# Queueing each product by V one softmax step later in a two-mixer encoder layer

## The chip, the cores and the metric

The kernel runs on one core of a Trainium2 chip. The metric is the device time of one execution in microseconds (us); less is better. All times below are of that core.

## What is computed

One encoder layer over 1024 frames of width 1024, with two token mixers, each with 8 heads of width 64. Mixer A is banded: a block of 128 queries sees at most 640 keys, with a learned bias. Mixer B is chunk-causal with a rotary part: the block of queries number i sees (i + 1) x 128 keys. Cut to what matters:

```python
# mixer A, per head and chunk
s = q @ k.T * scale + bias;  p = softmax(s);  y = p @ v
# mixer B, per head and block of 128 queries
s = q_full @ k_full.T * scale;  s = where(mask, s, -1e30);  p = softmax(s);  y = p @ v
# around them: projections of the layer's input, gates, output
ya = (y_A * silu(z_A)) @ w_proj_a
yb = (y_B * silu(z_B)) @ w_proj_b
out = (sigmoid(g_A) * ya + sigmoid(g_B) * yb) @ w_out, then a residual and a layer norm
```

## The kernel before, in words

The attention of a mixer is cut into 64 steps: 8 heads by 8 blocks of 128 queries, heads two by two in four "pairs", mixer A first (steps with `m` = 0), then mixer B (`m` = 1). One step (`Steps.one`) has these parts:

- `scores`: TensorE multiplies queries by keys into a tile of PSUM (pool `ps_sc`, two buffers); lines L692 and L693 for A, L789 to L791 for B. For A a step has 2 matmuls when i is under 4 and 4 otherwise; for B 3 and 6. VectorE moves the tile to SBUF and finds the row's extreme (L697 for A, L796 for B).
- `softmax`: ScalarE takes the exponential (L808), VectorE the reciprocal of the sum (L810, L811), ScalarE writes the upper half of the weights as fp16 (L815), VectorE the rest as a second fp16 part (L816). A transposing DMA, issued from SyncE (SP), brings both parts into a tile `pT` (L818).
- `pv`: the product by V. TensorE multiplies `v16` by `pT` (L830), two matmuls for each 128 keys of the step: 2, 4, 6, 8 and then 10 for A, 2 to 16 for B. They gather in a tile `y`, which holds four steps; after the fourth, `finish_y` evacuates it (L721, L722, L728) and stores it (L730).

The product by V of a step is not made in that step. `Steps` keeps a queue `q`; `fin` takes the oldest entry. With a lag of 3 (`LAG_A`) in A and 2 (`LAG_B`) in B, step s ends with the product of step s - 3 or s - 2. The pool of `pT` has lag + 1 buffers, so four in A and three in B. Besides, A has three buffers each for the scores in SBUF and for the fp16 weights, B two.

The steps are mixed with "dense" work: `run` interleaves the stream of steps with the stream of the big projections (`Chunk.mm`, six matmuls of 512 columns a unit, names `dn<-hT`, helper lines L167 to L169), by the share of each stream's cost that is done; the steps lead by a factor of 1.25. The order in which the program is written is a priority and not the final order: a planner puts each engine's instructions into a queue at compile time, taking the first in program order among those which it reckons to be ready. On the chip each engine works its queue off in that order, and waits on semaphores.

Between heads, `next_head` (at i = 6) starts the loads of the next head: the swapped queries `sX`, for A the bias tile `tb`, for B the rotary queries `qr`, of which there is one buffer. After A, `drain` makes the products that are left; after B the list `fins` does, interleaved with the projection of A (`proj_a`, name `pj`).

Of the kernel before, what the change touches and what calls it, by code (L numbers as in the profile page):

```python
# [18 lines left out]
P = 128  # L19
# [14 lines left out]
LAG_B = 2  # L34
# [21 lines left out]
def tile_hybrid_layer(  # L56
# [27 lines left out]
    T = nc.tensor  # L84

    def f(ap):
        return ap.bitcast(F32)
# [116 lines left out]
    def start_ya():  # L204

        if not YA:
            tiles = {}

            def one(k, half):
                if (k // 2, 0) not in tiles:  # L210
                    for a in range(2):
                        tiles[k // 2, a] = m8.tile([P, 2, S], F32R, tag="m8", name=f"YA{k // 2}{a}")
                for a in range(2):
                    YT[0][a] = YT[0][a] or {}
                    YT[0][a][k] = tiles[k // 2, a][:, k % 2, :]
                y_part(0, k, half, YT[0][0][k], YT[0][1][k])

            YA.extend([(0, lambda k=k, half=half: one(k, half)) for k in range(4) for half in range(2)])
        return YA

    def start_yb():

        t = [big.tile([P, 4, S], F32R, tag="big", name=f"YB{a}") for a in range(2)]
        for a in range(2):
            YT[1][a] = {k: t[a][:, k, :] for k in range(4)}
        return [(0, lambda k=k, half=half: y_part(1, k, half, YT[1][0][k], YT[1][1][k])) for k in range(3) for half in range(2)]
# [400 lines left out]
    with ExitStack() as p1:  # L627
# [24 lines left out]
        class PairA:  # L652
# [31 lines left out]
            def scores(self, e, i):  # L684
                h = 2 * self.p + e
                k0 = max(0, i - 4)
                n = (i - k0 + 1) * P
                ps = ps_sc.tile([P, 2, 512], F32, tag="sc", name=f"sa{h}_{i}")
                nb, w = (1, max(n, 256)) if n <= 512 else (2, n // 2)
                for b in range(nb):  # L690
                    ks = slice(k0 * P + b * w, k0 * P + b * w + w)
                    T.matmul(ps[:, b, :w], self.sQ[e][:, i * P : (i + 1) * P], self.sK[e][:, ks], start=True, stop=False)  # L692
                    T.matmul(ps[:, b, :w], self.sX[e][:, i * P : (i + 1) * P], self.sK[e][:, ks], start=False, stop=True)  # L693
                w = min(w, n)
                s = pools["s"].tile([P, 640], F32, tag="s", name=f"ss{h}_{i}")
                nm = sm.tile([P, 1], F32, tag="nm", name=f"nm{h}_{i}")
                V.tensor_tensor_reduce(  # L697
                    s[:, :n].rearrange("p (b w) -> p b w", b=nb),
                    ps[:, :nb, :w],
                    self.tb[e][:, 640 - n : 640].rearrange("p (b w) -> p b w", b=nb),  # L700
                    -0.125, 3e38, ALU.add, ALU.min, nm,
                )
                return s, nm, n
# [30 lines left out]
        class PairB:  # L734
# [46 lines left out]
            def scores(self, e, i):  # L781
                h = 2 * self.p + e
                n = (i + 1) * P
                ps = ps_sc.tile([P, 2, 512], F32, tag="sc", name=f"sb{h}_{i}")
                nb, w = (1, max(n, 256)) if n <= 512 else (2, n // 2)
                qs = slice(i * P, (i + 1) * P)
                for b in range(nb):
                    ks = slice(b * w, b * w + w)
                    T.matmul(ps[:, b, :w], self.sQ[e][:, qs], self.sK[e][:, ks], start=True, stop=False)  # L789
                    T.matmul(ps[:, b, :w], self.sX[e][:, qs], self.sK[e][:, ks], start=False, stop=False)  # L790
                    T.matmul(ps[:, b, :w], self.qr[e][:, qs], krt[:, ks], start=False, stop=True)  # L791
                w = min(w, n)
                V.memset(ps[0:64, nb - 1, w - 64 : w], NEG)
                s = pools["s"].tile([P, S], F32, tag="s", name=f"sbs{h}_{i}")
                nm = sm.tile([P, 1], F32, tag="nm", name=f"nmb{h}_{i}")
                V.tensor_scalar(  # L796
                    s[:, :n].rearrange("p (b w) -> p b w", b=nb), ps[:, :nb, :w], -B_SCALE, None,
                    op0=ALU.mult, op1=ALU.min, accum_out=nm,
                )
                return s, nm, n  # L800
# [1 line left out]
            def tail(self, e, half, yt, r):  # L802
                finish_z(self, 1, e, half, yt, r)

        def softmax(pair, e, i, nm_):
            s, nm, n = pair.scores(e, i)
            su = sm.tile([P, 1], F32, tag="su", name=f"su{nm_}")
            A.activation(s[:, :n], s[:, :n], AF.Exp, scale=-1.0, bias=nm, accum_out=su)  # L808
            rc2 = sm.tile([P, 1], F32, tag="rc2", name=f"rcs{nm_}")
            V.tensor_scalar(rc2, su, 2.0 ** -14, None, op0=ALU.mult)  # L810
            V.reciprocal(rc2, rc2)  # L811
            W_ = pools["w"]
            p16 = pools["p"].tile([P, 2 * W_], F16, tag="p16", name=f"p16{nm_}")
            hi, lo = p16[:, :n], p16[:, n : 2 * n]
            A.activation(hi, s[:, :n], AF.Copy, scale=rc2)  # L815
            V.scalar_tensor_tensor(lo, s[:, :n], rc2, hi, op0=ALU.mult, op1=ALU.subtract)  # L816
            pT = pools["pt"].tile([P, 2 * W_ // P, P], F16, tag="pt", name=f"pT{nm_}")
            SY.dma_start(pT[:, : 2 * n // P, :], p16[:, : 2 * n], transpose=True)  # L818
            return pT
# [18 lines left out]
        class Steps:  # L838
# [7 lines left out]
            def one(self):  # L846
                pair, e, i = self.seq[self.at]
                self.at += 1
                nm = f"{self.m}_{2 * pair.p + e}_{i}"
                self.q.append((pair, e, i, softmax(pair, e, i, nm)))  # L850
                if i == 6:
                    self.next_head()
                if len(self.q) > self.lag:
                    self.fin()

            def next_head(self):
                n = self.at + 1
# [70 lines left out]
        def att_pools(es, w, lag):  # L928
            pools["w"] = w
            for nm, bufs in (("s", 3 if w == 640 else 2), ("p", 3 if w == 640 else 2), ("pt", lag + 1)):  # L930
                pools[nm] = es.enter_context(tc.tile_pool(name=f"at_{nm}{w}", bufs=bufs, **rt))

        def at(units, where):

            out_ = []
            for i, u in enumerate(units):
                for w, more in where:
                    if w == i:
                        out_ += more
                out_.append(u)  # L940
            for w, more in where:
                if w >= len(units):
                    out_ += more
            return out_
# [21 lines left out]
        with ExitStack() as pb:  # L966
            att_pools(pb, S, LAG_B)
            pools["qr"] = pb.enter_context(tc.tile_pool(name="at_qr", bufs=1, **rt))
            krt = pools["qr"].tile([96, S], F32R, tag="kr", name="krt", bufs=1)
            for b, part in enumerate((0, 1, 0)):  # L970
                SY.dma_start(f(krt[32 * b : 32 * b + 32, :]), kr_d[part])
            pairsB[0].load_qr(0)
            sb = Steps(1, pairsB, LAG_B)
            for p in range(4):
                u = sb.units(16)
                if p < 3:
                    n = pairsB[p + 1]
                    extra = [(1 + j, [x_]) for j, x_ in enumerate(vb1[1])] if p == 0 else []
                    if p == 1:
                        extra = [(j, [x_]) for j, x_ in enumerate(vb1[2]())]  # L980
                    if p == 2:
                        extra = [(12 + j, [x_]) for j, x_ in enumerate(start_ya()[:4])]
                    u = at(u, extra + [(6, [(0, n.prep_w)]),
                               (PL[0], [(1.3, lambda n=n: n.prep_k(0))]), (PL[1], [(1.3, lambda n=n: n.prep_k(1))]),
                               (PL[2], [(1.3, lambda n=n: n.prep_q(0))]), (PL[3], [(1.3, lambda n=n: n.prep_q(1))])])
                    run(u, dense((5, 6, 5)[p]))
                else:
                    run(at(u[:5], [(j, [x_]) for j, x_ in enumerate(start_ya()[4:])]), dense(1))
                    yb = start_yb()
                    fins = [(0.5, sb.fin)] * LAG_B  # L990
                    run(at(u[5:] + fins, [(3 + j, [x_]) for j, x_ in enumerate(yb)]), proj_a(range(0, 6)))
            for _, fn in proj_a(range(6, 8)):
                fn()
# [94 lines left out]
    for j in range(NT):  # L1088
        n = 4 if j == last else 2
# [68 lines left out]
```

## Time and profile before

| what | value |
|---|---|
| median of 3 runs | 881.63 us (877.91 to 886.0) |
| profiled execution | 881.12 us |
| its span, first to last instruction | 879.3 us |
| mean granted clock of TensorE, as a share of full | 0.984 |
| attention of A, first scores to last product by V | 165.7 to 390.7 us |
| attention of B, first scores to last product by V | 377.0 to 725.9 us |

The profile shows one execution. PE is TensorE's matmuls, PEld its weight loads, DVE VectorE, ACT ScalarE, POOL GpSimd, SP SyncE with the DMA queue. A matmul's record ends at a modelled time; the next one often starts before that. A bracket behind a row holds the engine's idle time just before it and what ended that. A clock of 1.00 is 2.4 GHz, 0.50 is 1.2 GHz.

### The profile page before, as it was taken

Reading aid. Unit: us, or ns where it says so; the run is one execution under the profiler, and the core shown is the slowest. Engines: PE = TensorE matmul, PEld = TensorE weight load, DVE = VectorE, ACT = ScalarE, POOL = GpSimd, SP = SyncE. Lnnn points to the kernel's source line nnn. Section 1 sums busy time; section 2 is a strip of 40 time slices with the busy share of each in tenths; the row PEclk is TensorE's granted clock in tenths of the full one; section 3 lists DMA queues with packets and bytes.
Section 4 is the critical chain, followed back from the end, with each engine's and each line's share of the span. In section 5 each row is a group of like instructions: output and inputs, shape, how many; then the busy total and the mean of one; then the engine's idle time right before and its main releaser. Section 6 shows DMA issues by size and latency. Waiting matters only on the chain. (4 is left out here: it accounts for less than half of the span.)

```text
span 879.3 us, 13755 instructions
## 1 busy us (share of the span) xinstructions
PE 827.7 (94%) x4760; PEld 693.2 (79%) x4760; DVE 554.0 (63%) x1267; ACT 441.9 (50%) x857; POOL 299.6 (34%) x285
## 2 busy tenths in 40 slices
PE   4899799999998997899999999999999899999996
PEld 4899798887777775787787877888888778778886
DVE  6899765577667678846555645166527563557754
ACT  4233465377576756847553755366647452322000
POOL 5646642222232222712122732122344334541100
PEclk9999999999999998999999999999999899999998
DMA  6632103467878774685676566546877797541421
GB/s 193 207 120 76 37 24 96 152 131 149 171 136 178 143 147 108 121 195 117 138 159 154 128 142 144 162 106 150 212 186 181 153 220 255 184 149 59 146 96 48
DMA packets 185365, 124.68 MB, mean 142 GB/s; under 512 B 146160, under 2 KB 149744, under 8 KB 185296
## 3 DMA queue, kind: packets, MB, share of 16 engines
q1 hardware_dynamic: 185296, 123.82, 57.7%
q8 instruction: 37, 0.61, 0.3%
q14 instruction: 32, 0.26, 0.1%
HBM read 57.98 MB, written 22.81 MB: 92 GB/s over the span
## 5 line engine op out<-in xcount | busy, mean ns | idle before, releaser
L167 PE MATMUL dn<-hT,wh_c 128*128 128x512 f32 x512 | 204.7, 400 | 2.1 <-DVE bQ L640 1.0
L169 PE MATMUL dn<-hT,wl_c 128*128 128x512 f32 x512 | 201.3, 393 | 0.0
L168 PE MATMUL dn<-hT,wh_c 128*128 128x512 f32 x512 | 200.8, 392 | 0.0
L132 POOL TENSOR_TENSOR wl_c<-wr_c,wh_c 128x512 fp32r<-128x512 f32 x64 | 83.9, 1310 | 226.8 <-ACT wh_c L131 214.5
L167 PEld LDWEIGHTS dn<-hT,wh_c 128*128 128x128 f32 x512 | 96.7, 189 | 20.2 <-DVE bQ L640 1.4
L169 PEld LDWEIGHTS dn<-hT,wl_c 128*128 128x128 f32 x512 | 96.4, 188 | 19.7
L168 PEld LDWEIGHTS dn<-hT,wh_c 128*128 128x128 f32 x512 | 96.7, 189 | 17.5
L816 DVE SCALAR_TENSOR_TENSOR p<-sbs,rcs,p 128x128 f16<-128x128 f32 (+3 forms) x64 | 57.1, 898 | 28.3 <-ACT p L815 27.8
L728 POOL TENSOR_TENSOR yt<-yt,sz 64x512 f32<-64x512 f32 x32 | 43.2, 1349 | 92.8 <-DVE yt L722 62.9
L131 ACT ACTIVATE wh_c<-wr_c 128x512 fp32r<-128x512 f32 x64 | 40.2, 628 | 62.4 <-DMA wr_c<-in_wch_dram 49.1
L816 DVE SCALAR_TENSOR_TENSOR p<-ss,rcs,p 128x640 f16<-128x640 f32 (+2 forms) x64 | 54.6, 867 | 19.8 <-ACT p L815 18.9
L808 ACT ACTIVATE sbs<-sbs,nmb 128x128 f32<-128x128 f32 (+3 forms) x64 | 49.4, 772 | 31.4 <-DVE sbs L796 26.1
L808 ACT ACTIVATE ss<-ss,nm 128x640 f32<-128x640 f32 (+2 forms) x64 | 44.3, 692 | 29.3 <-DVE nm L697 22.6
L810 DVE TENSOR_SCALAR rcs<-su 128x1 f32<-128x1 f32 x128 | 19.3, 152 | 62.4 <-ACT sbs L808 45.2
L815 ACT ACTIVATE p<-sbs,rcs 128x128 f16<-128x128 f32 (+3 forms) x64 | 48.8, 771 | 13.0 <-ACT sbs L808 7.2
L167 PE MATMUL ops<-wo,mixT 128*128 128x512 f32 (+1 forms) x144 | 51.7, 372 | 1.2 <-ACT wo L131 1.1
L169 PE MATMUL ops<-wo,mixT 128*128 128x512 f32 (+1 forms) x144 | 52.5, 367 | 0.0
L168 PE MATMUL ops<-wo,mixT 128*128 128x512 f32 (+1 forms) x144 | 52.2, 366 | 0.0
L796 DVE TENSOR_SCALAR_CACHE_REDUCE sbs<-sb 128x128 f32<-128x128 f32 (+3 forms) x64 | 47.9, 755 | 1.5
L830 PE MATMUL y<-pT,v16a 128*128 128x128 f16 x480 | 39.0, 223 | 10.2 <-DMA pT<-p 10.2
L830 PE MATMUL y<-pT,v16b 128*128 128x128 f16 x576 | 44.7, 220 | 3.9 <-DMA pT<-p 3.9
L830 PEld LDWEIGHTS <-v16b 128*128 128x128 f16 x576 | 33.0, 98 | 18.8 <-issue 16.2
(247 smaller groups left out, 1895.0 us busy)
## 6 DMA issues: line engine op xcount, KB each, us to landing
wr_c<-in_wch_dram SPq DMA_DIRECT2D x64, 256.0 KB, 3.0
th_d<-g SPq DMA_DIRECT2D x32, 256.0 KB, 2.6
th<-th_d SPq DMA_DIRECT2D x32, 256.0 KB, 3.9
h_d<-xt SPq DMA_DIRECT2D x8, 512.0 KB, 2.8
sX<-sQ SPq DMA_DIRECT2D x16, 256.0 KB, 4.2
sXb<-bQ SPq DMA_DIRECT2D x16, 256.0 KB, 3.8
r<-h_d SPq DMA_DIRECT2D x8, 512.0 KB, 4.0
wor<-in_wo_dram SPq DMA_DIRECT2D x16, 256.0 KB, 3.3
```

The lines of the kernel that those rows point to most:

```text
L131: A.activation(hi, raw, AF.Copy)
L132: (eng or V).tensor_tensor(lo, raw, f(hi), op=ALU.subtract)
L167: T.matmul(ps, ah, bh, start=start, stop=False)
L168: T.matmul(ps, ah, bl, start=False, stop=False)
L169: T.matmul(ps, al, bh, start=False, stop=stop)
L728: G.tensor_tensor(yt[r, :], yt[r, :], pair.sz[half][r, :], op=ALU.mult)
L796: V.tensor_scalar(s[:, :n].rearrange("p (b w) -> p b w", b=nb), ps[:, :nb, :w], -B_SCALE, None, op0=ALU.mult, op1=ALU.min, accum_out=nm,)
L808: A.activation(s[:, :n], s[:, :n], AF.Exp, scale=-1.0, bias=nm, accum_out=su)
L810: V.tensor_scalar(rc2, su, 2.0 ** -14, None, op0=ALU.mult)
L815: A.activation(hi, s[:, :n], AF.Copy, scale=rc2)
L816: V.scalar_tensor_tensor(lo, s[:, :n], rc2, hi, op0=ALU.mult, op1=ALU.subtract)
L830: T.matmul(o, v16[:, k0 + k, h % 4, :], pT[:, a * nk + k, :], start=(k == 0 and a == 0), stop=(k == nk - 1 and a == 1))
```

## The change

In a step, the scores come first; then, if more than `lag` entries wait, the product by V of the oldest; then the softmax of the step. The entry of the step itself is added last, so that the product that step s makes is now that of step s - 4 in A and s - 3 in B. `issue_after(pair.last)` puts all of its matmuls (and nothing of other engines) behind the last matmul of the step's scores in TensorE's queue; it is an order only, with no wait for a result. The pools are as before: `pT` has four buffers in A and three in B. `drain` has one product more, and so has the list `fins`.

```diff
-                    T.matmul(ps[:, b, :w], self.sX[e][:, i * P : (i + 1) * P], self.sK[e][:, ks], start=False, stop=True)
+                    self.last = T.matmul(ps[:, b, :w], self.sX[e][:, i * P : (i + 1) * P], self.sK[e][:, ks], start=False, stop=True).ins
...
-                    T.matmul(ps[:, b, :w], self.qr[e][:, qs], krt[:, ks], start=False, stop=True)
+                    self.last = T.matmul(ps[:, b, :w], self.qr[e][:, qs], krt[:, ks], start=False, stop=True).ins
...
-        def softmax(pair, e, i, nm_):
-            s, nm, n = pair.scores(e, i)
+        def softmax(s, nm, n, nm_):
...
-                self.q.append((pair, e, i, softmax(pair, e, i, nm)))
+                sc = pair.scores(e, i)
+                if len(self.q) > self.lag:
+                    with tc.issue_after(pair.last):
+                        self.fin()
+                self.q.append((pair, e, i, softmax(*sc, nm)))
                 if i == 6:
                     self.next_head()
-                if len(self.q) > self.lag:
-                    self.fin()
...
-                    fins = [(0.5, sb.fin)] * LAG_B
+                    fins = [(0.5, sb.fin)] * (LAG_B + 1)
```

## Rows read from the trace of the kernel before

**Rows 1.** The page: busy time, share of the span and instructions of each engine.

```profile
PE 827.7 (94%) x4760; PEld 693.2 (79%) x4760; DVE 554.0 (63%) x1267; ACT 441.9 (50%) x857; POOL 299.6 (34%) x285
```

**Rows 2.** Timeline of TensorE, two dense matmuls: start, length, line, operation.

```profile
299.80 0.39 PE L167 MATMUL dn<-hT,wh_c 128*128 128x512 f32 x1
300.03 0.39 PE L168 MATMUL dn<-hT,wh_c 128*128 128x512 f32 x1
```

**Rows 3.** TensorE's waits: line, who ended them; us in total, times, longest.

```profile
PE y L830 <- DMA pT<-p: 14.1, 21, 1.7
...
PE sb L791 <- DMA qr<-qr_d: 2.3, 2, 1.6
PE sa L692 <- DVE sK L643: 2.1, 1, 2.1
```

**Rows 4.** The tile pT: its transposes (ns, min/median/max), time to landing (us).

```profile
L818 SPq DMA_TRANSPOSE pT<-p x128: 1167/1338/4564, 178.7 to 720.5; - x128
...
DMA to landing us min/median/max: 2.3/3.4/6.5
```

**Rows 5.** Timeline of TensorE, products by V that waited, with scores behind them.

```profile
229.65 0.27 PE L830 MATMUL y<-pT,v16a 128*128 128x128 f16 x2 [0.84 <-DMA pT<-p]
229.73 0.47 PE L169 MATMUL dn<-hT,wl_c 128*128 128x512 f32 x1
...
230.51 0.39 PE L169 MATMUL dn<-hT,wl_c 128*128 128x512 f32 x1
230.74 0.30 PE L692 MATMUL sa<-sK,sQ 128*128 128x320 f32 x1
...
231.17 0.30 PE L693 MATMUL sa<-sK,sX 128*128 128x320 f32 x1
```

**Rows 6.** Timeline of TensorE, a product that waited with its scores ahead.

```profile
688.18 0.34 PE L789 MATMUL sb<-bK,bQ 128*128 128x384 f32 x1
...
692.00 1.05 PE L830 MATMUL y<-pT,v16b 128*128 128x128 f16 x16 [1.73 <-DMA pT<-p]
```

**Rows 7.** Timeline of TensorE at three changes of head.

```profile
318.93 0.73 PE L830 MATMUL y<-pT,v16a 128*128 128x128 f16 x10
...
327.75 0.62 PE L830 MATMUL y<-pT,v16a 128*128 128x128 f16 x8
330.43 0.38 PE L692 MATMUL sa<-sK,sQ 128*128 128x256 f32 x1 [2.06 <-DVE sK L643]
...
423.40 0.90 PE L830 MATMUL y<-pT,v16b 128*128 128x128 f16 x13
425.85 0.38 PE L791 MATMUL sb<-krt,qr 96*128 96x256 f32 x1 [1.55 <-DMA qr<-qr_d]
...
508.17 0.90 PE L830 MATMUL y<-pT,v16b 128*128 128x128 f16 x13
509.79 0.38 PE L791 MATMUL sb<-krt,qr 96*128 96x256 f32 x1 [0.73 <-DMA qr<-qr_d]
```

**Rows 8.** Timeline of VectorE, then of SP, for one softmax of mixer B.

```profile
645.27 0.11 DVE L793 MEMSET sb<- 64x64 f32 x1 [3.37 <-PE sb L791]
...
647.15 0.35 DVE L816 SCALAR_TENSOR_TENSOR p<-sbs,rcs,p 128x128 f16<-128x128 f32 x1 [0.52 <-ACT p L815]
...
647.57 1.22 SPq L818 DMA_TRANSPOSE pT<-p  x1
```

**Rows 9.** Windows: stretch, its length, busy PE, PEld, DVE, ACT, POOL; clock, DMA.

```profile
350.00:355.00 5.00, 3.92 (x16) 2.51 (x17) 4.92 (x13) 3.90 (x10) 3.91 (x6) 0.50 0.91 159
...
690.00:695.00 5.00, 3.10 (x26) 2.65 (x24) 3.05 (x10) 3.51 (x10) 2.55 (x2) 0.88 0.83 225
695.00:700.00 5.00, 4.33 (x13) 2.99 (x13) 3.62 (x12) 3.77 (x7) 2.46 (x2) 0.50 0.28 59
700.00:705.00 5.00, 5.00 (x27) 4.29 (x25) 4.99 (x7) 2.19 (x4) 2.95 (x3) 0.93 0.70 139
```

## The prediction

> **What bounds the kernel now.** I read the page's busy line first: PE 94%, the next engine DVE 63% [rows 1]. TensorE is the one engine whose idle time can cost; the reader should look for gaps on it and forget the long idle times of the others. Busy hides a little, though. Two dense matmuls of 512 columns start 0.23 us apart while each record is 0.39 us long [rows 2], so the last 0.16 us of a record is overlapped when work follows at once and is lost when TensorE has to wait. A wait therefore costs its bracket plus about 0.16 us.
>
> The Trainium skill says the same of such records: its page "Perfetto Trace Analysis", Identifying the Most-Contended Engine, calls matmul busy time a poor measure and wants weight-load busy instead. That row stands at 79% [rows 1]; taken at its word it would leave 879.3 - 693.2 = 186 us of headroom, while the dense rows, spaced as they are, show almost none. Here the rows decide.
>
> Next, TensorE's waits [rows 3]. Products by V that waited for the transposed weights `pT` are the largest entry: 14.1 us in 21 waits, longest 1.7. With 21 x 0.16 = 3.4 us of drain that is 17.5 us, or 2% of the span: the whole prize of this change. The other entries of that view (operands of scores at a change of head, weights) are not touched by it.
>
> Why they wait: a transposing DMA lands 3.4 us after its issue in the median, but up to 6.5 us [rows 4]. The planner put the product where it reckoned the tile to be there, and the chip was later by 0.2 to 1.7 us.
>
> **Part one: the product goes behind one more set of scores.** What matters is not "one step" but what TensorE gets to do in between, and that depends on where the product already stood. I went through the 21 waits in the timeline, counting matmuls to find each one's step, and looked for the scores of four steps later (A) or three (B).
>
> In 11 of the 21 these scores still stood behind the waiting product. The pattern: the product at 229.65 waited 0.84 us; then came four dense matmuls, and then the scores of four steps later, the last at 231.17 [rows 5]. After the change all of that, 1.6 us, goes first, and the wait is gone. For 8 of these 11 the work that goes first is longer than the wait; for three (at 254.08, 279.86 and 369.13) it covers 0.5 to 0.7 us of it. In sum 4.1 us of waits vanish wholly and 1.8 us in part; with 8 x 0.16 of drain, 4.1 + 1.8 + 1.3 = **7.2 us gained**.
>
> In the other 10 (8.1 us of waits) the order is already what the change asks for, or the product is one of the last, in `fins`. The largest: the scores of three steps later stand at 688.18, the product waits at 692.00 for 1.73 us [rows 6]. Pinning it behind 688.18 moves nothing. It stays where the planner thinks its tile has landed, and I leave these 8.1 us in. Bounds: none of them gained, or all with their drain, 8.1 + 13 x 0.16 = 10.2 us (the three that are covered in part included; with what is left of those, 1.1 us, it is 11.3).
>
> **Part two: the same buffers.** The transpose of step s now needs the buffer that the product of the same step frees. Before, that product stood ahead of the scores; now it is right behind. SP works in order, so a transpose that waits holds the weight loads behind it. The tightest chain I found: scores are out at 645.27, VectorE finishes the weights at 647.15 + 0.35 = 647.50, the transpose starts at 647.57 [rows 8]. So TensorE has 2.2 us after the scores. The product takes (0.90 - 0.22) / 12 = 0.057 us a matmul (13 in 0.90 us, the last record 0.22 long [rows 7]), at most 16 x 0.057 = 0.9 us. It hides under the softmax with 1.3 us to spare; elsewhere that softmax takes 5 us and more. I cost this at nothing. If the cover is gone, each us lands on SP and on the softmax, not on TensorE at once. The fp16 weights are freed when the transpose has read them, as before.
>
> **Part three: products pinned at a change of head.** The new order takes away filler. When the first scores of a head cannot start, the last four (A) or three (B) products of the head before used to run; now they must stay behind those scores. Three places show it [rows 7]: at 318.93 and 327.75 products (18 matmuls, 18 x 0.057 = 1.0 us) ran ahead of scores that then waited 2.06 us for keys; at 423.40 and 508.17, 13 matmuls (0.7 us each) ran ahead of waits of 1.55 and 0.73 us for `qr`. If nothing else is put there, these waits get longer by 1.0 + 0.7 + 0.7 = 2.4 us; if the planner puts dense matmuls there instead, by nothing. It plans with such matmuls ready nearly everywhere, but it did not foresee these waits. I take the middle, **1.2 us lost**, bounds 0 and 2.4.
>
> **Part four: moved along.** Per four steps, `finish_y` (L721, L722, L728, a store on SP) comes one step later; its result is read back only much later, except for the last head. There `fins` has three entries instead of two, in the order that stood in the queue anyway, so nothing. `drain` makes four products with `pT` in place for three of them: nothing. No instruction is added or removed on any engine.
>
> **Sum.** 881.1 (profiled execution, 1.8 us over its span) - 7.2 + 1.2 = 875.1 us. The median of the runs is 0.5 us above that execution, so 875.5 us. Own range of this case: 871 to 880, from a gain of 10 (part of the other waits) to one of 2 (bounds of part three, and a new wait or two).
>
> **Rivals.**
>
> *All waits go.* If one step more of distance lets every `pT` land in time, 17.5 us are gained. Besides, the granted clock returns: after the idle time at 690 to 692 us it is 0.50 from 695 to 700 and part of the windows beside it, (1 - 0.88) x 10 + 5 + (1 - 0.93) x 10 = 6.9 us at 1.2 GHz [rows 9], which costs half of the busy part, about 3.0 us. The like stretch at 350 to 355 would give 2.5. Then 881.6 - 17.5 to 23 = 859 to 864 us. For it: the waits are short, 0.7 us in the mean, against 3.5 us a step in A (225 us for 64 steps). Against it: the 10 places of part one, and the clock at 350 falls by other waits too.
>
> The page "TensorE: Matmul & The Clock Gate" of the Trainium skill, under Why this matters for your kernels, warns against gaps between bursts of matmuls for the clock's sake; the 0.50 behind the gap at 692 agrees.
>
> *The queue hardly changes, or what is gained comes back.* The planner orders everything anew from its own reckoning; places that were covered may get waits of the same size, as 107 products of 128 have none now, many with little to spare. Then 878 to 885, about 881.
>
> *Slower: the pins starve TensorE at changes of head.* There are 15. At each, four products of 10 matmuls (40 x 0.057 = 2.3 us) in A, or 12 + 14 + 16 = 42 (2.4 us) in B, are locked behind scores that wait for a DMA or an evacuation. It decides from the point at which no dense matmul is ready in that gap. If five of the 15 lose 2.3 us, and two of the longer gaps bring a stretch at 1.2 GHz of 3.0 us each, the loss is 11.5 + 6 = 17.5; less the gain, 881.6 - 7.2 + 17.5 = 892 us. For it: such waits are already second and third in the view [rows 3] and one is 2.06 us. Against it: in most changes of head dense matmuls filled the gap.
>
> **How the numbers follow.** Forecast 0.44, all waits go 0.15, little change 0.24, slower 0.17. About 1% (8.8 us) is what a measurement of this kernel can tell from no change. Faster by over 1% means under 872.8: the second case and some 0.17 of chance from the forecast's lower part, 0.32. Slower by over 1% means over 890.4: most of the slower case and a little of what the planner may do, 0.17. Within 1%: 0.51. The range runs from inside the second case to the slower one, 862 to 892, with 2 in 10 left out.
>
> **What would show it.** Right: in TensorE's waits the entry for `pT` falls from 14.1 to about 8 us, its count from 21 to about 13; in the timeline L693 or L791 stands directly ahead of most L830; the waits at a change of head grow by 1 to 2 us; transposes still start within 0.1 us of L816's end. Wrong: the entry falls to nearly nothing (first rival), keeps its size in other places (second), or waits of scores for keys or `qr` grow to 10 us with more stretches at 0.50 (third). Transposes that start long after L816 would show that part two was mispriced.

## The result and the profile after

The changed kernel takes 887.9 us in the median of 13 runs (885.75 to 889.36), the kernel before 880.83 us (877.91 to 886.0) on the same chip: ratio 1.0065, 95% interval 1.005 to 1.0079. It is slower by 7 us where about 6 us of gain were forecast. The profiled execution took 888.73 us. Ratios here and below leave out two executions in a slow state, of 1356.8 and 2185.9 us.

No instruction was added, and TensorE's busy time moved little against [rows 1]. The busy line of the page after:

```profile
PE 831.1 (94%) x4760; PEld 698.4 (79%) x4760; DVE 554.9 (63%) x1267; ACT 443.2 (50%) x857; POOL 300.8 (34%) x285
```

Its span and mean granted clock, which were 879.3 us and 0.984:

```profile
core 0: 886.9 us, clock 0.980
```

From the line of the exponential on, lines of the changed kernel count one less. TensorE's waits after (line, who ended them; us in total, times, longest):

```profile
PE y L829 <- DMA pT<-p: 14.0, 18, 2.2
...
PE sa L692 <- DVE nm L697: 6.1, 3, 2.8
PE sb L789 <- DVE sbs L796: 3.5, 2, 3.2
...
PE sb L791 <- DMA qr<-qr_d: 2.9, 2, 1.8
...
PE sa L692 <- DVE sK L643: 1.9, 1, 1.9
```

Beside [rows 3]: the products' entry did not fall (14.1 before), only its count did, and the longest is longer. What is new are scores that wait for VectorE, 9.6 us in the second and third row; these two entries were 1.5 and 0.2 us before.

To sum over the attention I took all of TensorE's waits over 0.17 us from 160 to 745 us, by what waited. Before: products 14.1 us, scores 6.2, other 4.8, sum 25.1. After: 14.1, 14.4, 0.8, sum 29.3. That is 4.2 us of the 7.6 by which the span grew. The rest is about what the clock cost. Windows after (stretch, length, busy PE, PEld, DVE, ACT, POOL; clock, DMA):

```profile
285.00:289.00 4.00, 4.00 (x14) 2.82 (x13) 3.75 (x11) 3.21 (x7) 1.29 (x1) 0.57 0.50 97
353.00:360.00 7.00, 5.41 (x13) 4.44 (x14) 6.81 (x15) 6.24 (x14) 6.12 (x7) 0.54 0.69 131
387.00:391.00 4.00, 3.56 (x18) 3.07 (x18) 0.70 (x1) 0.42 (x1) 0.41 (x1) 0.58 0.90 220
664.00:671.00 7.00, 5.67 (x14) 4.22 (x15) 4.95 (x15) 4.51 (x10) 4.84 (x5) 0.51 0.47 137
```

By the trace's clock records TensorE stood at 1.2 GHz for 23.9 us of the attention, against 17.1 before; an estimate is that half of the difference, 3.4 us, is lost. Each of the four windows lies at one of the four longest waits: 283.94 (2.61 us), 354.59 (2.79), 387.44 (2.25, a product) and 665.25 (3.20). The one at 353 has its like in the kernel before, at 350 [rows 9]; the one at 695 there is gone.

Where the first of these waits comes from can be followed over four engines. Timeline after: TensorE, ScalarE, VectorE and SP before 284 us:

```profile
283.94 0.41 PE L692 MATMUL sa<-sK,sQ 128*128 128x320 f32 x1 [2.61 <-DVE nm L697]
...
280.04 0.42 ACT L131 ACTIVATE wh_vb<-wr_vb 128x256 fp32r<-128x256 f32 x1 [5.82 <-DMA wr_vb<-in_wvb_dram]
...
282.34 0.51 ACT L807 ACTIVATE ss<-ss,nm 128x256 f32<-128x256 f32 x1
...
274.57 0.41 DVE L697 CUSTOM_DVE_ANT_0 ss<-sa,tb 128x256 f32<-128x256 f32 x1
...
280.49 0.42 DVE L132 TENSOR_TENSOR wl_vb<-wr_vb,wh_vb 128x256 fp32r<-128x256 f32 x1 [5.50 <-ACT wh_vb L131]
...
282.35 0.75 DVE L643 SCALAR_TENSOR_TENSOR sK<-dn,bcol,sK 64x512 fp32r<-64x512 f32 x1 [1.36 <-ACT sK L642]
...
283.31 0.56 DVE L697 CUSTOM_DVE_ANT_0 ss<-sa,tb 128x384 f32<-128x384 f32 x1
...
271.50 4.16 SPq L817 DMA_TRANSPOSE pT<-p  x2
275.75 0.84 SPq L730 DMA_DIRECT2D y_d<-yt  x1
276.65 0.58 SPq L135 DMA_DIRECT2D wr_vb<-in_wvb_dram  x1
```

Read it from below. SP issues a weight load at 276.65, behind two transposes (4.16 us) and a store. ScalarE has come to that weight's split and stands 5.82 us; VectorE stands 5.50 us behind it for the other half. Then VectorE waits 1.36 us more, for ScalarE's half of an evacuation of keys (`sK`). The reduction that empties a score tile (L697) starts at 283.31, and the next scores, which need that PSUM tile, only then. In the kernel before the same load was issued 1.3 us earlier, ahead of a transpose and the store, and ScalarE did not stand for it. It stood 2.81 us for another weight just before, so about 3 us of the 5.82 are new. Timeline of SP and of ScalarE, kernel before:

```profile
275.38 0.43 SPq L135 DMA_DIRECT2D wr_vb<-in_wvb_dram  x1
275.92 1.56 SPq L818 DMA_TRANSPOSE pT<-p  x1
277.57 0.60 SPq L730 DMA_DIRECT2D y_d<-yt  x1
...
278.29 0.63 ACT L131 ACTIVATE wh_c<-wr_c 128x512 fp32r<-128x512 f32 x1 [2.81 <-DMA wr_c<-in_wch_dram]
...
279.32 0.40 ACT L131 ACTIVATE wh_vb<-wr_vb 128x256 fp32r<-128x256 f32 x1
```

The wait at 665.25 is the same from ScalarE on, with the weight `wr_p`. Timeline after, TensorE, then ScalarE, VectorE, SP, GpSimd:

```profile
665.25 0.76 PE L789 MATMUL sb<-bK,bQ 128*128 128x512 f32 x1 [3.20 <-DVE sbs L796]
665.82 0.63 PE L790 MATMUL sb<-bK,sXb 128*128 128x512 f32 x1
666.24 0.63 PE L791 MATMUL sb<-krt,qr 96*128 96x512 f32 x1
666.95 0.26 PE L829 MATMUL y<-pT,v16b 128*128 128x128 f16 x1
...
662.41 0.63 ACT L131 ACTIVATE wh_p<-wr_p 128x512 fp32r<-128x512 f32 x1 [3.11 <-DMA wr_p<-in_wpa_dram]
...
663.36 1.16 DVE L815 SCALAR_TENSOR_TENSOR p<-sbs,rcs,p 128x128 f16<-128x128 f32 x1 [3.68 <-ACT p L814]
...
659.73 0.33 SPq L135 DMA_DIRECT2D wr_p<-in_wpa_dram  x1
...
658.41 1.29 POOL L132 TENSOR_TENSOR wl_c<-wr_c,wh_c 128x512 fp32r<-128x512 f32 x1 [4.09 <-ACT wh_c L131]
```

No transpose stands ahead of this load; SP starts none between 648.25 and 664.60 us. The load goes out 0.03 us after GpSimd ends its half of an earlier weight's split (658.41 + 1.29 = 659.70), which until then holds a buffer of the same pool (`wp`). So a weight can be late with no transpose ahead of it, here by all appearance for want of a buffer.

The wait at 354.59 has no late weight in it: VectorE is at work on other things in its queue. Timeline after, TensorE, then VectorE:

```profile
354.59 0.66 PE L692 MATMUL sa<-sK,sQ 128*128 128x384 f32 x1 [2.79 <-DVE nm L697]
...
351.95 1.44 DVE L815 SCALAR_TENSOR_TENSOR p<-ss,rcs,p 128x640 f16<-128x640 f32 x1 [0.37 <-ACT p L814]
353.43 0.68 DVE L640 TENSOR_TENSOR bK<-bk,bK 64x512 fp32r<-64x512 f32 x1
354.14 0.29 DVE L697 CUSTOM_DVE_ANT_0 ss<-sa,tb 128x128 f32<-128x128 f32 x1
```

In the rows at 665 us the new order can be seen as well: the product (L829) stands directly behind the scores (L791). So the change does what it says. The question is why that brings nothing.

### The profile page after: what moved, and what is told of

Read it like the earlier page. It is cut to its first block, busy times and chain, and to the rows that moved or that the text cites. A ratio compares the mean times of both kernels' runs of the same rounds, so it can differ in the third digit from the quotient of the medians.

```text
span 886.9 us, 13730 instructions
## 1 busy us (share of the span) xinstructions
PE 831.1 (94%) x4760; PEld 698.4 (79%) x4760; DVE 554.9 (63%) x1267; ACT 443.2 (50%) x857; POOL 300.8 (34%) x285
## 5 line engine op out<-in xcount | busy, mean ns | idle before, releaser
L167 PE MATMUL dn<-hT,wh_c 128*128 128x512 f32 x512 | 208.6, 408 | 0.8 <-DVE bK L640 0.8
L168 PE MATMUL dn<-hT,wh_c 128*128 128x512 f32 x512 | 203.6, 398 | 0.0
L169 PE MATMUL dn<-hT,wl_c 128*128 128x512 f32 x512 | 203.5, 397 | 0.0
L167 PEld LDWEIGHTS dn<-hT,wh_c 128*128 128x128 f32 x512 | 98.5, 192 | 19.0 <-DVE bK L640 1.2
L168 PEld LDWEIGHTS dn<-hT,wh_c 128*128 128x128 f32 x512 | 98.4, 192 | 18.1
L815 DVE SCALAR_TENSOR_TENSOR p<-ss,rcs,p 128x640 f16<-128x640 f32 (+2 forms) x64 | 57.5, 912 | 19.7 <-ACT p L814 18.9
L829 PE MATMUL y<-pT,v16b 128*128 128x128 f16 x576 | 44.3, 220 | 6.4 <-DMA pT<-p 6.3
L829 PEld LDWEIGHTS <-v16b 128*128 128x128 f16 x576 | 33.3, 98 | 20.6 <-issue 18.8
L814 ACT ACTIVATE p<-ss,rcs 128x640 f16<-128x640 f32 (+2 forms) x64 | 42.9, 688 | 10.2 <-DMA pT<-p 4.5
L809 DVE TENSOR_SCALAR rcs<-su 128x1 f32<-128x1 f32 x128 | 19.2, 151 | 45.1 <-ACT sbs L807 32.2
```

What stands on the lines that cost most here:

```text
L167: T.matmul(ps, ah, bh, start=start, stop=False)
L168: T.matmul(ps, ah, bl, start=False, stop=False)
L169: T.matmul(ps, al, bh, start=False, stop=stop)
L829: T.matmul(o, v16[:, k0 + k, h % 4, :], pT[:, a * nk + k, :], start=(k == 0 and a == 0), stop=(k == nk - 1 and a == 1))
```

## The experiments

All ratios are to the kernel before, run on the same chip; they compare all executions and can differ from the quotient of two medians by up to 0.3%. First theory: the edit makes the planner order every queue anew, and some weight loads land late ("new plan", later "late weights"). Rivals: the pins themselves; the buffers; and, from the fifth run on, that any new plan of this kernel is a draw, the kernel before being a good one ("scatter"), or that the new order costs time by itself ("the order itself costs"). Waits are of one profiled execution for each kernel; executions of the kernel before alone took 875.5 to 888.2 us.

**One part at a time.** e1: no pins.

```diff
-                    with tc.issue_after(pair.last):
-                        self.fin()
+                    self.fin()
```

> The changed kernel without the order edges: the product by V of the older step is still written behind the scores, but the planner may put it ahead of them. Theory 'new plan' (the products cost nothing where they are; the new plan puts weight loads later on SP, and ScalarE and VectorE stand behind a weight load): 884 to 891 us, TensorE's waits of scores for VectorE (L692 and L789) 6 to 12 us in all, the clock at 0.50 in about as many stretches. Theory 'pins' (products locked behind scores starve TensorE): 876 to 881, those waits back to about 2 us. Theory 'buffers' (transposes wait for a pT that is freed later): 882 to 886, since without the pin the product may run before the scores, and transposes start within 0.1 us of L815's end.

890.11 us, ratio 1.0087 (1.0058 to 1.0116); waits of products 16.5 us, of scores 13.4. That is in the range of the new plan; without pins the kernel is no faster, so they are not the cost.

e2 and e3: the new order in mixer A alone (`self.m == 0 and ...`, elsewhere the old place), or in B alone.

> The new order in mixer A alone, mixer B as before. The changed kernel's loss of 7.6 us in the span lies with 3 us between 160 and 395 us and 5 us between 395 and 730 us. If each mixer's order costs by itself: 883 to 885. Theory 'new plan': the sum need not hold; 878 to 889, and what it costs is seen in waits of L692 for VectorE at about 284 and 354 us, with a stretch at 0.50 behind each. Theory 'pins': 883 to 885 with the waits at changes of head.

> The new order in mixer B alone, mixer A as before. If each mixer's order costs by itself: 885 to 887, with a wait of L789 for VectorE of about 3 us near 665 us. Theory 'new plan': 878 to 889; A's plan is the one of before, so the first 390 us should agree with it within 0.5 us, and what B costs hangs on the place of its weight loads. Theory 'pins': 885 to 887, waits for qr above 2.9 us.

885.18 us, 1.0028 (1.0006 to 1.005), and 889.64 us, 1.008 (1.0053 to 1.0106). Both lie above what each mixer's order by itself should cost, and the two do not add up to the whole change: 0.28 + 0.80 is more than 0.65%. With the new order in A alone the scores wait 11.6 us, with it in B alone 13.2.

e4: the old lag and the old place, but pinned behind the scores of its own step.

> The old order and lag with the pin alone: a product is queued behind the scores of the step that made it due in the old program, one step earlier than in the change. Theory 'pins': slower than before by a part of the change's loss, 883 to 888. Theory 'new plan': the old program order is kept and most products stood behind these scores anyway, so the plan hardly moves: 879 to 884. Theory 'buffers': as before, 880 to 882.

886.36 us, 1.0048 (1.0022 to 1.0075). An order that asks for almost what the old one had costs about three quarters of the whole difference (0.48 of 0.65%). By the expectation this is the range of the pins (883 to 888), not that of the new plan, which should hardly have moved (879 to 884). Against the pins stands e1 alone.

**One stall taken away, and more room.** e5: the load of `wr_vb` is asked for three steps earlier (the expectation says four); the queues change little elsewhere.

```diff
-                if p == 2:
+                if p == 1:
                     v0, v1, v2 = vb_group(0)
-                    u = at(u, [(1, v0)] + [(4 + 2 * j, [x_]) for j, x_ in enumerate(v1)])
+                    u = at(u, [(14, v0)])
+                if p == 2:
+                    u = at(u, [(4 + 2 * j, [x_]) for j, x_ in enumerate(v1)])
```

> The changed kernel, with one weight load (for V of the second mixer, group 0) asked for four steps earlier, so that it stands ahead of three transposes and a store on SP; only some 100 lines of SP's queue and a tenth of PE's differ from the changed kernel. Late weights (the reordered queues put a load late, ScalarE and VectorE stand behind its split, the scores behind them, and the clock halves): the wait of 2.61 us at L692 near 284 us and the half-clock stretch of 3.4 us near 285 us both go, the products' waits for pT stay near 14, and 2.5 to 4.5 us come back: 883.5 to 885.5 us, ratio to the kernel before 1.003 to 1.005. Scatter of plans (any change of order lands somewhere between 0 and +0.9%): those two may go as well, but others come elsewhere, and the time stays at 886 to 889. The order itself costs (products late, buffers held): no change, 887 to 889.

889.6 us, 1.008 (1.006 to 1.0101): no gain, where late weights called for 883.5 to 885.5. Timeline of e5, SP, then ScalarE and TensorE:

```profile
273.67 4.77 SPq L817 DMA_TRANSPOSE pT<-p  x2
278.54 0.77 SPq L730 DMA_DIRECT2D y_d<-yt  x1
279.36 0.58 SPq L679 DMA_DIRECT2D tb<-in_relb_dram  x1
280.04 0.39 SPq L135 DMA_DIRECT2D wr_c<-in_wch_dram  x1
...
283.41 0.63 ACT L131 ACTIVATE wh_c<-wr_c 128x512 fp32r<-128x512 f32 x1 [7.33 <-DMA wr_c<-in_wch_dram]
...
279.36 0.44 PE L829 MATMUL y<-pT,v16a 128*128 128x128 f16 x5 [2.00 <-DMA pT<-p]
...
285.37 0.41 PE L692 MATMUL sa<-sK,sQ 128*128 128x320 f32 x1 [1.36 <-DVE nm L697]
```

The load of `wr_vb` is out of the way, and the next one in line, `wr_c`, is late behind the same two transposes: ScalarE now stands 7.33 us. The scores' wait fell from 2.61 to 1.36 and a product waits 2.00 us instead. The slow clock moves as well. Windows of e5:

```profile
285.00:290.00 5.00, 3.88 (x19) 3.13 (x20) 4.36 (x15) 3.87 (x8) 1.42 (x2) 1.00 0.43 103
310.00:315.00 5.00, 4.78 (x26) 4.10 (x26) 4.27 (x14) 4.82 (x9) 1.17 (x1) 0.67 0.30 58
```

The stretch at 285 is gone, and one at 311 has come. Over the attention TensorE's waits rose from 29.3 to 33.2 us, while its time at 1.2 GHz fell from 23.9 to 13.7 us. So the chain of late weights is real at this place, but mending one link of it was worth nothing.

e6 and e7: eight buffers for dense weights instead of seven, in the new and in the old order (`wp` 7 to 8; `sm` 6 to 4, `ln_p2` 6 to 2 and `st6o` 3 to 2 make the room).

> The changed kernel with eight instead of seven buffers for the dense weights (room made by smaller rings for scalars), so that a load need not wait for the chunk before to release one. Late weights: ScalarE's waits for wr_c fall from 64 us to below 50, the scores' waits sa<-nm and sb<-sbs fall from 9.6 to below 4, and the time falls to 880 to 884, below the same edit on the kernel before plus 2 us. Scatter: 882 to 890, with waits elsewhere. The order itself costs: still 5 to 8 us above the same edit on the old order.

> The kernel before with the same eight weight buffers. Late weights: its loads are in time already, so 879 to 883 (ratio 0.997 to 1.002). Scatter: 881 to 889, slower than the kernel before by up to 0.9%. The order itself costs: 5 to 8 us below the changed kernel with the same edit.

New order 895.43 us, 1.0152 (1.0131 to 1.0173); old order 885.76, 1.0046 (1.0027 to 1.0066). More room for weights made both slower, the new order most. The first theory, as I had put it (880 to 884 us), falls here. The 895.43 us lie above the range of scatter too, and the 9.7 us between the pair came nearest to what the order itself should cost (5 to 8). What the smaller rings cost by themselves was not run.

e12: one more `pT` buffer in A (`lag + 1 + (w == 640)`).

> The changed kernel with one more buffer for pT in the first mixer (five instead of four), so that a transpose need not wait for the product four steps back. Buffers as the cost (products later in the same buffers hold the transposes): the waits for pT fall from 14 to below 10 us and the time by 2 to 4, 884 to 886. Late weights or scatter: only the end of the first mixer is ordered anew, waits for pT stay at 12 to 16 us, 886.5 to 890.

887.49 us, 1.0093 (1.0062 to 1.0124), the waits for `pT` 16.8 us. Buffers are not the cost in A; in B a fourth was not tried.

**An edit that does not touch the products.** `LEAD`, 1.25 in both kernels, is how far the steps of the attention run ahead of the dense work. I changed it alone, in both orders:

```diff
-LEAD = 1.25
+LEAD = 1.2
```

> The kernel before, with the attention stream let run 1.20 instead of 1.25 times ahead of the dense stream: an edit that has nothing to do with products and their scores, but reorders every queue. Scatter of plans: slower by 0.2 to 0.9%, 882.5 to 889. Late weights or the order itself as the only cost: the old order stays within 0.2%, 879 to 883.

> The changed kernel with the attention stream's lead 1.20, to stand beside the old order with the same lead (889.58 us, ratio 1.0093). Scatter of plans: the new order has no cost of its own, so within 4 us of that, on either side: 885.5 to 893.5. The order itself costs: 5 to 8 us above it, 895 to 898. A gain of the new order hidden by the re-plan: 2 us or more below it, under 887.5.

> The changed kernel with the lead 1.30. Scatter of plans: anywhere from 882 to 895, within 4 us of the old order with the same lead, sign open. The order itself costs: 5 to 8 us above the old order with 1.30.

> The kernel before with the lead 1.30. Scatter of plans: 0.2 to 0.9% slower than with 1.25, as 1.20 was: 884 to 890. If the lead of 1.20 was slower for less lead and not for a new plan: at or below the kernel before, 878 to 882.

> The changed kernel with the lead 1.23, close under the 1.25 of both kernels. If the new order has an effect of its own under the scatter of plans, it has the same sign here as at 1.20 and 1.30 (-10 and -9 us against the old order with the same lead): 3 to 12 us below the old order with 1.23. If the effect is scatter alone: a difference of either sign, up to 10 us.

> The kernel before with the lead 1.23. If the kernel before stands on a plan that happens to be good at 1.25 alone: 883 to 893 us, slower by 0.2 to 1.3%. If it is good in a neighbourhood: 878 to 883.

> The changed kernel with the lead 1.27, close above 1.25. An effect of its own: 3 to 12 us below the old order with 1.27. Scatter alone: either sign, 878 to 895 us.

> The kernel before with the lead 1.27. A good plan at 1.25 alone: 883 to 895 us. Good in a neighbourhood: 878 to 883.

With e6 and e7 and the two kernels themselves that makes six pairs that differ in the change alone. Ratios to the kernel before with their intervals, and TensorE's waits of products and of scores (us, 160 to 745 us, as above):

| setting | old order | new order | products old, new | scores old, new |
|---|---|---|---|---|
| lead 1.20 | 1.0093 (1.0068 to 1.0118) | 0.9971 (0.9941 to 1.0000) | 19.0, 14.5 | 7.6, 6.1 |
| lead 1.23 | 0.9991 (0.9967 to 1.0015) | 1.0019 (0.9995 to 1.0043) | 18.5, 16.1 | 5.6, 10.2 |
| lead 1.25 | 1 | 1.0065 (1.005 to 1.0079) | 14.1, 14.1 | 6.2, 14.4 |
| lead 1.27 | 1.0094 (1.0065 to 1.0124) | 1.0109 (1.0061 to 1.0157) | 22.9, 21.9 | 5.6, 9.8 |
| lead 1.30 | 1.0223 (1.0175 to 1.0272) | 1.0122 (1.007 to 1.0173) | 24.6, 19.2 | 6.9, 7.4 |
| eight weight buffers | 1.0046 (1.0027 to 1.0066) | 1.0152 (1.0131 to 1.0173) | 16.1, 15.6 | 4.8, 14.8 |

Three things are to be seen. The change moves the time by -1.2, +0.3, +0.65, +0.15, -1.0 and +1.1%: mean 0.0%, standard deviation 0.9%. At 1.20 and 1.30 the new order is 9 to 10 us faster, which e9's expectation gave to a hidden gain; at 1.23 and 1.27 it is 1 to 2 us slower, which that gain (3 to 12 us) excludes. The mean of six is known to about 0.4%, so a gain of 0.7%, as forecast, is neither shown nor excluded. Products wait less or as long in all six, 2.3 us less in the mean ((19.0 + 18.5 + 14.1 + 22.9 + 24.6 + 16.1 - 14.5 - 16.1 - 14.1 - 21.9 - 19.2 - 15.6) / 6). Scores wait more in five of six, 4.3 us more in the mean; the other waits lose 1.5 us. (The standard errors of the two means are 0.9 and 1.8 us.) So on average the change moves waits from products to scores, and at 1.25 only the second half happened, as 14.1 us is the lowest value of the products that any old order has. The entries of two of these runs, where the change gains most; TensorE's waits of the old order with 1.20, then of the new:

```profile
PE y L830 <- DMA pT<-p: 19.3, 28, 2.4
...
PE sa L692 <- DVE nm L697: 2.5, 2, 2.3
```

```profile
PE y L829 <- DMA pT<-p: 14.5, 22, 2.0
...
PE sa L692 <- DVE nm L697: 3.2, 5, 1.2
```

Not all of this need be scatter. The lead may have a best value of its own, near 1.24 for the old order and lower for the new; then a pair at one lead compares two places of two curves. The edits that leave the lead alone moved the time by less: e4 and e7 by 0.5% on the old order, e1, e5 and e12 by 0.15 to 0.3% on the new, only e6 by 0.9%.

**A smaller lead for the new order.** The old order is fastest at 1.23 to 1.25, the new one still gained at 1.20.

> The changed kernel with the lead 1.18. With the new order the time so far falls with the lead all the way: ratio 1.012 at 1.30, 1.011 at 1.27, 1.0065 at 1.25, 1.002 at 1.23, 0.997 at 1.20, while the old order is best near 1.24. If the new order wants a smaller lead (a trend): at or below 1.20's, ratio 0.990 to 0.998, 873 to 881 us, faster than both kernels. If 1.20 was one lucky plan: 1.000 to 1.010, 882 to 891.

> The changed kernel with the lead 1.15. Trend: ratio 0.987 to 0.998, or turning up again past the best, up to 1.003. One lucky plan at 1.20: 1.000 to 1.010, 882 to 891 us.

At 1.18: 876.53 us, ratio 0.9917 (0.9888 to 0.9947), faster than both kernels. At 1.15: 885.02 us, 1.0025 (0.9999 to 1.0052). Over the lead, 1.15, 1.18, 1.20, 1.23, 1.25, 1.27, 1.30, the new order gives 885.0, 876.5, 879.3, 884.5, 887.9, 892.2, 891.8 us: nearly a smooth valley, its floor 0.05 or so below the old order's. That it is a valley is not shown: at 1.15 the time lies in the ranges of both expectations, and the 1.1% between 1.18 and 1.15 is as large as the differences of the pairs, so 1.18 may also be a lucky plan. TensorE's waits at 1.18:

```profile
PE y L829 <- DMA pT<-p: 17.9, 14, 2.3
PE sa L692 <- DVE nm L697: 1.7, 2, 1.3
```

The products wait longer than in either kernel and the scores hardly at all. To see the whole account I took, for each matmul, the time to the next one's start and took off the 30th percentile of this spacing over all matmuls of the same shape (30% stand as close or closer). What is left over is lost time; it holds waits and slow clock alike. Each row is one execution; that of 1.15 took 890.01 us, 5 us over the median of its runs.

| us | packed matmuls | lost before A | in A | in B | after B | lost in all | span |
|---|---|---|---|---|---|---|---|
| kernel before | 786.3 | 25.3 | 31.3 | 22.3 | 4.1 | 83.0 | 879.3 |
| changed kernel | 786.6 | 25.2 | 34.4 | 27.4 | 3.2 | 90.2 | 886.9 |
| old order, 1.20 | 786.6 | 23.9 | 36.0 | 28.3 | 3.1 | 91.3 | 888.0 |
| new order, 1.20 | 786.3 | 24.2 | 30.8 | 24.6 | 1.4 | 81.0 | 877.4 |
| new order, 1.18 | 786.4 | 24.5 | 26.8 | 26.4 | 1.3 | 79.0 | 875.6 |
| new order, 1.15 | 787.6 | 25.9 | 33.3 | 29.8 | 1.4 | 90.4 | 888.2 |

The work is the same everywhere within 1.3 us; the spans differ mostly by what is lost in A and B.

## Why the prediction was wrong

**What bounds the kernel** held: TensorE's gaps decide, and the account above finds 7.2 of the 7.6 us there.

**Part one** is the step that failed. It put the products' entry at about 8 us and 13 waits, a gain of 7.2; measured were 14.0 us and 18, a gain of 0.1. The order did come out as I had it: the median product starts 1.04 us (A) and 1.31 us (B) before the end of the scores behind which it should go in the kernel before, and 0.15 us before the end of their last record after, which is directly behind them, as records overlap. The time from a step's scores to its product grew from 12.73 to 14.10 us in A and from 14.02 to 16.61 in B, while the chain in between, up to the landing of `pT`, took 11.73 to 11.99 and 11.05 to 11.67. The mean slack between landing and product doubled in A (1.0 to 2.1 us) and grew from 3.0 to 4.9 us in B, and yet products that started within 0.3 us of the landing went from 20 to 17 in A and from 10 to 14 in B.

Step by step, the cover came: of the 11 waits that part one wanted to cover (8.0 us) ten are gone, and 0.25 us is left of the eleventh. Of the other ten, four are left (1.6 us before, 3.5 after). But 13 products that had not waited now do, for 10.2 us. So what failed is that I followed the 21 waits of one plan into another as if all else stayed: the 107 products without a wait, which the rival "what is gained comes back" names, stood at nothing in the sum. The products that wait after the change have hardly a longer chain than the rest (12.0 us from scores to landing, against 11.8 in the mean of all); they start 12.0 us after their scores, where the mean of all is 15.4. The new plan gave more distance on average, but not to these; why the planner gives it so unevenly is open. In the six pairs the term is 2.3 us, not 7.2.

There is also a slip in the working: the other ten waits hold 6.1 us, and 8.1 is what the 7.2 us leave of all the waits, without the drain. The 7.2 does not hang on it; the upper bound of 11.3 counts what is left of the three twice.

**The term that was missing** is the scores' waits: +8.2 us here, +4.3 in the mean of the pairs. I had priced scores only at a change of head (part three).

**Part two**: right in its price, nothing. Transposes start 0.07 us after VectorE's second half in the median, before and after; e12 agrees for A. But the cover was not everywhere: two transposes in B, at 433.44 and 518.95 us, start 0.03 us after the product that frees their buffer, 1.25 and 2.09 us after VectorE had ended. In the kernel before there is no such case. TensorE's next wait comes more than 50 us after either, so the price stands.

**Part three**: 1.2 us was too much. At the three places of [rows 7] the waits were 2.06, 1.55 and 0.73 us, sum 4.34; after they are 1.86, 1.15 and 1.76, sum 4.77, so 0.4, which is within the bounds of 0 to 2.4. Timeline after:

```profile
332.20 0.39 PE L692 MATMUL sa<-sK,sQ 128*128 128x256 f32 x1 [1.86 <-DVE sK L643]
...
426.43 0.39 PE L791 MATMUL sb<-krt,qr 96*128 96x256 f32 x1 [1.15 <-DMA qr<-qr_d]
...
510.55 0.39 PE L791 MATMUL sb<-krt,qr 96*128 96x256 f32 x1 [1.76 <-DMA qr<-qr_d]
```

**Part four** was not tried by itself: what is lost after B went from 4.1 to 3.2 us.

**The rivals.** "All waits go" is refuted. "The pins starve TensorE" gave a time nearer to the measured one, but its mechanism is not there: e1 without pins is no faster. "What is gained comes back" had the mechanism, and its reach of 878 to 885 was too short. It did not reckon with this, that the kernel before is a good plan among its like: of the six old orders only the one with 1.23 comes level, the four others are 0.5 to 2.2% slower. Whether that is luck or a well-chosen lead is not shown.

**Still open**: whether and why the new order wants a smaller lead. That its scores wait less there (2.8 us at 1.18, against 14.4) fits, but they wait 11.4 us at 1.15 and 7.4 at 1.30, so the lead does not set it alone. The old order was not run at 1.18; the gain of 0.8% belongs to order and lead together.

## What to carry to other kernels

Where a planner orders the queues, an edit's price cannot be read off the waits of one trace: first make two or three edits that should change nothing, and take their spread (here 0.5% with e4 and e7, up to 2.2% with the lead) as the least that a single comparison must exceed. A wait that is gone says nothing of the places that had none: count the new waits too. Compare the two versions at several settings of a constant that both have, each at its own best as well. When a wait on the bottleneck is mended, look for what stands next in the same queue; here the next load took the place of the one that was moved.

## What the runs showed of the hardware

A transposing DMA holds SP's queue for long and unevenly. After the change the eight of B's largest step (1024 keys) hold it 1.86 to 4.66 us each, those of at most 512 keys 1.17 to 1.98 us. At 271.50 two of them took 4.16 us, and the weight load that stood behind them was late. The tile `pT` after (transposes in ns, min/median/max; time to landing), beside [rows 4]:

```profile
L817 SPq DMA_TRANSPOSE pT<-p x128: 1167/1337/4663, 178.6 to 728.7; - x128
...
DMA to landing us min/median/max: 2.3/3.6/8.2
```

The Trainium skill, page "DMA: Bandwidth & Descriptors", Issuing engines are not separate DMA queues, calls the time that it takes to initiate a DMA usually small beside the DMA itself. For these transposes the trace differs: the median one holds SP 1.34 us where the median time to the landing is 3.6 us, and the longest holds it 4.66 us.

ScalarE stood 5.82 us for one weight, and VectorE 5.50 us for ScalarE's half of it. Behind that weight the exponential of a step stood in ScalarE's queue; VectorE had ended its input by 275.0 us, and it ran at 282.34. The Trainium skill, page "Perfetto Trace Analysis", Tensor Engine Instruction, calls ScalarE and VectorE strictly first in, first out; the rows at 280 us agree.
